# One stationary for the beta/decay projection, reordered opening transfers, chunk work by halves, and single row loads in the tail

## The chip, the cores and the metric

The kernel runs on one core of one Trainium2 chip. The metric is the device time of one execution in microseconds, the median of several runs. TensorE (PE) does matrix products into PSUM, VectorE (DVE), ScalarE (ACT) and GpSimd (POOL) do the elementwise work, SyncE (SP) issues transfers; ScalarE and GpSimd can issue transfers as well. Each engine works through its own queue in order, and a transfer that has to wait holds up all that stands behind it in the queue that issues it.

## What is computed

One layer of a hybrid decoder on 1024 prompt tokens and 8 x 4 sample tokens (1056 columns in all), model width 1024, 8 heads of 128. All is fp32. The parts that matter here:

```python
u = _rmsnorm(x, norm_w)
proj = jnp.einsum('btd,dn->btn', u, w_in)
a_b, a_c, a_h, a_z, qkv, b_z, b_beta, b_alpha, g_a, g_b = jnp.split(proj, _split_points(), axis=-1)
...
qkv_c, new_qkv_buf = _causal_conv(qkv, conv_qkv_buf, conv_b_w)      # width 4, per channel
qkv_c = jax.nn.silu(qkv_c).astype(jnp.float32)
...
beta = jax.nn.sigmoid(b_beta)
g = -jnp.exp(a_log) * jax.nn.softplus(b_alpha + dt_bias)
o, S_new = _gated_delta(q, k, v, beta, g, S0)                       # chunked; decays L, products k k^T and q k^T
...
m = jax.nn.sigmoid(g_a) * y_a + jax.nn.sigmoid(g_b) * y_b
return x + jnp.einsum('btd,de->bte', m, w_o), new_a_buf, new_qkv_buf, S_new
```

`b_beta` and `b_alpha` are 8 columns each, so the beta/decay projection has 16 columns where every other unit has 128.

## The kernel before

Every fp32 product is made of three products at reduced precision: each operand is split into a high part (`uh`, `wh`) and a low part (`ul`, `wl`), and `wh*uh + wl*uh + wh*ul` is accumulated (L286). A unit of the input projection is 128 weight columns: 8 row blocks x 3 products x 3 column blocks of 352 tokens, 72 matmuls. `fetch_plain` (L177) loads its weights on SP's queue, `prep` (L184) makes `wh` on ScalarE (L188) and `wl` on VectorE (L190). `take` (L212) prepares up to two units ahead and fetches up to four ahead, as the buffers allow (three raw weight tiles `wr`, four split tiles `hl`).

In the opening (L435 to L468) nine blocks of x rows are loaded on SP, squared on ScalarE, scaled with `nwb` (the norm weights on all partitions, loaded by a broadcast on ScalarE's queue, L437) on VectorE (L455), transposed on TensorE (L460) and split into `uh` and `ul`. Then come the beta/decay unit (BA) and the first key unit (k0), block by block in turn (L466), and the unpacking of BA (L471 to L567), which gives `beta`, the gates and their running sums. These go to DRAM (`gscr`, L546) and are read back per head by a broadcast, as `ee` and `qd` (L590, L594).

The head loop (L788) runs the convolution of k, q and v for each of eight heads: a projection, an evacuation by ScalarE (L404), edge columns by GpSimd (L411 to L414), and the taps on ScalarE and VectorE (L416, L418). `decay_matrices` (L596) turns `ee` into the decays: GpSimd (L599), VectorE (L600), ScalarE (L601). The work of a head on its chunks is the generator `chunk` (L715). `pump()` is called after each of the nine blocks of a head and takes one step of the chunk of the head before; `finish(fore)` runs what is left of it. `chunk` has ten steps: `qd` and two stores; the eight transposes of k with squares and scalings (L733, L734); the norms (`tk`, `al`, `bp`); the squares of q; and for each half the products (L756), the masks, the stores of `mm` into three scratch tensors (L768 to L774), the transposes of v and the store of `pk` (L784). The clearing stores of the scratch tensors (L801, 1 MB each) go out on SP two per head in heads 0 to 4.

Afterwards come the unit products of z, then pairs of units in a seven-product scheme (`project_pair`, L311), each pair 7 x 24 matmuls, with the inversion, the merge, the scan and the sample stage as `background` steps between the products. Ahead of the last gate pair (L1220) the background is run to its end, and five `y` rows are loaded at once on ScalarE's queue (L1226). The output projections follow.

The order in each queue is planned ahead by a scheduler that simulates the program's times, so instructions of neighbouring steps can change places. The plan is fixed when the program is built.

## Time and profile before

| | us |
|---|---|
| median of three runs | 1457.48 (1456.57 to 1462.76) |
| the profiled execution | 1458.91 |
| its span | 1457.2 |
| TensorE busy | 1393.4 (96%) |
| VectorE busy | 793.8 (54%) |
| ScalarE busy | 550.9 (38%) |
| GpSimd busy | 408.6 (28%) |

The span lies 1.7 us under the time of the execution. An engine's busy time counts its instructions, not its waits. The granted clock is the share of TensorE's full speed of 2.4 GHz: 1.00 is full speed, 0.50 is the lower level of 1.2 GHz. Matmuls overlap each other, so the duration of one is longer than its share of the time; how fast they follow is read from the time that a known number of them takes. "Queue" lines with a q behind the engine (SPq, ACTq) are the issue of a transfer, not the transfer.

### The profile page before, as it was taken

Reading aid. Unit: us, or ns where it says so; the run is one execution under the profiler, and the core shown is the slowest. Engines: PE = TensorE matmul, PEld = TensorE weight load, DVE = VectorE, ACT = ScalarE, POOL = GpSimd, SP = SyncE. Lnnn points to the kernel's source line nnn. Section 1 sums busy time; section 2 is a strip of 40 time slices with the busy share of each in tenths; the row PEclk is TensorE's granted clock in tenths of the full one; section 3 lists DMA queues with packets and bytes.
Section 4 is the critical chain, followed back from the end, with each engine's and each line's share of the span. In section 5 each row is a group of like instructions: output and inputs, shape, how many; then the busy total and the mean of one; then the engine's idle time right before and its main releaser. Section 6 shows DMA issues by size and latency. Waiting matters only on the chain.

```text
span 1457.2 us, 24544 instructions
## 1 busy us (share of the span) xinstructions
PE 1393.4 (96%) x9673; PEld 1339.5 (92%) x9673; DVE 793.8 (54%) x1456; ACT 550.9 (38%) x1184; POOL 408.6 (28%) x613
## 2 busy tenths in 40 slices
PE   4999898998999999899999999999999899999998
PEld 3899898998999999799999999999988899999785
DVE  6255543455438998455545566466676462355322
ACT  5165545555543443133334443442232440123111
POOL 2034323132211100475444565542253000001100
PEclk8999999999999999999999999999999999999999
DMA  6167755655546235944355776654446773333311
GB/s 202 29 141 205 188 164 171 195 135 145 135 136 152 87 106 128 227 91 120 81 144 156 212 201 196 183 161 124 116 134 196 256 247 100 103 118 109 142 44 47
DMA packets 229124, 212.33 MB, mean 146 GB/s; under 512 B 45801, under 2 KB 200314, under 8 KB 229010
## 3 DMA queue, kind: packets, MB, share of 16 engines
q1 hardware_dynamic: 204224, 139.91, 34.5%
q0 software_dynamic: 21712, 64.10, 15.0%
q10 hardware_dynamic: 3074, 6.77, 1.3%
q8 instruction: 76, 1.25, 0.3%
q14 instruction: 38, 0.31, 0.1%
HBM read 138.12 MB, written 72.56 MB: 145 GB/s over the span
## 4 chain that ended last, share of the span: by engine, by line
PE 68%; DMA 12%; DVE 11%; issue 3%; SPq 3%; POOL 1%; ACT 1%; DVEq 0%; POOLq 0%; ACTq 0%
PE pb L325 27%; PE pp L287 24%; PE pp L1319 6%; DMA ee<-gscr 6%; DMA wr<-in_w_in_dram 2%; DVE cv L418 2%; DMA sb<-in_state_delta_dram 1%; DVE wl L190 1%; DMA ya<-in_x_prompt_dram 1%; DVE xi L620 1%; PE pd L1021 1%; DVE pr L619 1%; PE po L1147 1%; PE pd L1145 1%; PE pd L756 1%
## 5 line engine op out<-in xcount | busy, mean ns | idle before, releaser
L325 PE MATMUL pb<-uh,w 128*128 128x264 f32 x1600 | 312.1, 292 | 12.1 <-ACT w L208 5.8
L325 PEld LDWEIGHTS pb<-uh,w 128*128 128x128 f32 x1600 | 253.5, 191 | 17.3 <-ACT w L208 7.2
L287 PE MATMUL pp<-uh,wl 128*128 128x352 f32 (+1 forms) x744 | 243.1, 327 | 14.0 <-DVE wl L190 14.0
L287 PE MATMUL pp<-uh,wh 128*128 128x352 f32 (+1 forms) x744 | 250.0, 336 | 3.3 <-ACT ext L406 3.3
L287 PE MATMUL pp<-ul,wh 128*128 128x352 f32 (+1 forms) x744 | 242.7, 326 | 0.0
L325 PE MATMUL pb<-ul,w 128*128 128x264 f32 x800 | 232.1, 290 | 0.0
L287 PEld LDWEIGHTS pp<-uh,wl 128*128 128x128 f32 (+1 forms) x744 | 139.9, 188 | 18.5 <-DVE wl L190 16.0
L325 PEld LDWEIGHTS pb<-ul,w 128*128 128x128 f32 x800 | 153.1, 191 | 1.7 <-issue 1.7
L287 PEld LDWEIGHTS pp<-uh,wh 128*128 128x128 f32 (+1 forms) x744 | 139.5, 188 | 7.3 <-ACT ext L406 3.7
L287 PEld LDWEIGHTS pp<-ul,wh 128*128 128x128 f32 (+1 forms) x744 | 139.8, 188 | 2.2
L208 ACT CAST w<-s 128x512 fp32r<-128x512 f32 x100 | 61.5, 620 | 139.1 <-PE pb L325 97.8
L418 DVE SCALAR_TENSOR_TENSOR cv<-ext,vecT,cv 128x1080 f32<-128x1080 f32 x72 | 99.7, 1388 | 9.7 <-ACT cv L416 8.3
L209 DVE TENSOR_TENSOR w<-s,w 128x512 fp32r<-128x512 f32 x100 | 72.2, 723 | 32.6 <-ACT w L208 32.2
L188 ACT CAST wh<-wr 128x1024 fp32r<-128x1024 f32 (+1 forms) x47 | 48.7, 1036 | 107.6 <-PE pp L287 105.2
L325 PE MATMUL pb<-t4h,w 128*128 128x264 f32 x400 | 78.8, 295 | 5.0 <-DVE p L858 5.0
L190 DVE TENSOR_TENSOR wl<-wr,wh 128x1024 fp32r<-128x1024 f32 (+1 forms) x47 | 59.8, 1272 | 37.3 <-ACT wh L188 36.2
L325 PE MATMUL pb<-t7h,w 128*128 128x264 f32 x400 | 77.6, 291 | 0.0
L325 PE MATMUL pb<-t6h,w 128*128 128x264 f32 x400 | 77.2, 289 | 0.0
L209 DVE TENSOR_TENSOR w<-wr,w 128x512 fp32r<-128x512 f32 x75 | 51.3, 686 | 45.2 <-ACT w L208 45.1
L325 PEld LDWEIGHTS pb<-t4h,w 128*128 128x128 f32 x400 | 64.2, 194 | 6.4 <-issue 6.4
L208 ACT CAST w<-wr 128x512 fp32r<-128x512 f32 x75 | 46.7, 623 | 52.5 <-PE pb L325 50.2
L331 ACT COPY p<-pb 128x528 f32<-128x528 f32 x50 | 30.0, 600 | 92.7 <-PE pb L325 92.7
(366 smaller groups left out, 3148.7 us busy)
## 6 DMA issues: line engine op xcount, KB each, us to landing
wr<-in_w_in_dram SPq DMA_DIRECT2D x80, 512.0 KB
scr<-pk SPq DMA_DIRECT2D x16, 768.0 KB
sb<-in_state_delta_dram POOLq DMA_DIRECT2D x16, 512.0 KB, 4.4
zscr<-zt SPq DMA_DIRECT2D x8, 528.0 KB
gbscr<-zt SPq DMA_DIRECT2D x8, 528.0 KB
yscr<-za SPq DMA_DIRECT2D x8, 528.0 KB
gascr<-zt SPq DMA_DIRECT2D x8, 528.0 KB
sg<-gascr POOLq DMA_DIRECT2D x8, 528.0 KB, 4.0
```

Of the source, the lines that this page charges most:

```text
L188: act.copy(wh, wr)
L190: dve.tensor_tensor(wl, wr, wh.bitcast(F32), op=ALU.subtract)
L208: act.copy(w2[:, 0], src)
L209: dve.tensor_tensor(w2[:, 1], src, w2[:, 0].bitcast(F32), op=ALU.subtract)
L287: pe.matmul(ps[:a.shape[2], :BLK], lhsT=a[:, k, :], rhs=m[k][:, sl], start=(k == 0 and i == 0), stop=(k == KC - 1 and i == 2))
L325: pe.matmul(ps[:, g, :QT], lhsT=a[:, k, :], rhs=m[:, k, sl], start=start and k == 0 and i == 0, stop=(k == 3 and i == 2), skip_group_check ...
L331: act.copy(t, ps)
L418: dve.scalar_tensor_tensor(cv, ext[:, j:j + LB], vecT[:, j * 24 + ci:j * 24 + ci + 1], cv, op0=ALU.mult, op1=ALU.add)
L619: dve.tensor_tensor(pv, xi[:, 0:j, 0:j], bc(dl[:, j, 0:j], 1, [P, j, j]), op=ALU.mult)
L620: dve.tensor_reduce(xi[:, 0:j, j], pv, axis=AX.X, op=ALU.add, negate=True)
L756: pe.matmul(pt[:, i * 256:(i + 1) * 256], lhsT=kq[:, 0, c * P:(c + 1) * P], rhs=kq[:, :, c * P:(c + 1) * P], start=True, stop=True)
L1319: pe.matmul(ps[:n, :], lhsT=a[k][:, sl], rhs=w[k][:, cs_], start=(k == 0 and i == 0), stop=(k == KC - 1 and i == 2))
```

## The change

Six things are changed. The weights of BA become one tile of 48 columns, with the high part in columns 0 to 15, zeros in 16 to 31 and the low part in 32 to 47; two products take the place of three, and the two results are added when BA is unpacked. The norm weights are loaded as one row and spread over the partitions by two products with `ones`. BA and k0 are taken without looking ahead; the next units are fetched behind the rows of x. `ee` and `qd` are loaded, and `mm` is stored, on GpSimd's queue (`aux`). `chunk` does all of one half before the other, in nine steps. The five `y` rows are loaded on GpSimd's queue, one per product of the last gate pair, by a new generator.

```diff
@@ -184,6 +184,12 @@
     def prep(u, j):
         if u[0] == "c":
             wr, n = rawc.pop(j) if j in rawc else fetch_plain(u)
+            if n == 16:
+                both = wp.tile([P, KC, 48], F32R, tag="hl", name="wb", bufs=4)
+                pool.memset(both[:, :, 16:32].bitcast(F32), 0.0)
+                act.copy(both[:, :, 0:16], wr)
+                dve.tensor_tensor(both[:, :, 32:48], wr, both[:, :, 0:16].bitcast(F32), op=ALU.subtract)
+                return both, None
             wh = wp.tile([P, KC, n], F32R, tag="hl", name="wh", bufs=4)
             act.copy(wh, wr)
             wl = wp.tile([P, KC, n], F32R, tag="hl", name="wl", bufs=4)
@@ -283,6 +289,11 @@
 
         def mm(ps, b, k):
             sl = slice(b * BLK, (b + 1) * BLK)
+            if wl is None:
+                for i, (n, m) in enumerate(((48, mh), (16, ml))):
+                    pe.matmul(ps[:n, :BLK], lhsT=wh[:, k, 0:n], rhs=m[k][:, sl], start=(k == 0 and i == 0),
+                              stop=(k == KC - 1 and i == 1), skip_group_check=True)
+                return
             for i, (a, m) in enumerate(((wh, mh), (wl, mh), (wh, ml))):
                 pe.matmul(ps[:a.shape[2], :BLK], lhsT=a[:, k, :], rhs=m[k][:, sl], start=(k == 0 and i == 0),
                           stop=(k == KC - 1 and i == 2))
@@ -394,7 +405,7 @@
     s_st, st = opened(name="st", bufs=1, side="right")
     s_y, pools["y"] = opened(name="xy", bufs=1, side="right")
 
-    def conv_begin(ci):
+    def conv_begin(ci, ahead=True):
         ext = qe.tile([P, EXB], F32, name="ext", bufs=2)
         sv = psel(ext, 3 + T, NT + 3, 3)
 
@@ -404,7 +415,7 @@
             act.copy(ext[:, 3 + lo:3 + lo + n], ps[:, :n])
             if b == NBLK - 1:
                 act.copy(sv[:, :, 3:7], ps[:, n:n + TS].rearrange("p (b t) -> p b t", t=NT))
-        mm, run = begin(w_in, C_Q + ci * P, uh, ul)
+        mm, run = begin(w_in, C_Q + ci * P, uh, ul, ahead)
         return ext, sv, run, evac
 
     def conv_end(ci, out, ext, sv):
@@ -433,14 +444,19 @@
         return xt
 
     xts = [load_x(0), load_x(1), load_x(2)]
+    nwr = st.tile([1, D], F32, tag="pq", name="nwr", bufs=2)
+    nc.scalar.dma_start(nwr, norm_w)
     nwb = ytile(7, (P, D))
-    nc.scalar.dma_start(nwb, norm_w[0].partition_broadcast(P))
-    _, run_ba = begin(w_in, C_BA, uh, ul)
-    ext_k0, sv_k0, run_k0, evac_k0 = conv_begin(8)
-    bar = st.tile([16, TT], F32, name="bar")
+    for i in range(2):
+        pt = dtile()
+        pe.matmul(pt, lhsT=ones[0:1, :], rhs=nwr[:, i * 512:(i + 1) * 512], start=True, stop=True)
+        dve.tensor_copy(nwb[:, i * 512:(i + 1) * 512], pt)
+    _, run_ba = begin(w_in, C_BA, uh, ul, False)
+    ext_k0, sv_k0, run_k0, evac_k0 = conv_begin(8, False)
+    bar = st.tile([48, TT], F32, name="bar")
 
     def evac_ba(b, ps):
-        act.copy(bar[:, b * BLK:(b + 1) * BLK], ps[:16, :BLK])
+        act.copy(bar[:, b * BLK:(b + 1) * BLK], ps[:48, :BLK])
 
     for tb in range(9):
         n = P if tb < 8 else TS
@@ -463,6 +479,9 @@
             pv = pt.rearrange("p (k t) -> p k t", t=P)[:, :, :n]
             act.copy(gh, pv)
             dve.tensor_tensor(gl_, pv, gh.bitcast(F32), op=ALU.subtract)
+    ready[pos[0]] = prep(units[pos[0]], pos[0])
+    for j in range(1, 3):
+        rawc[pos[0] + j] = fetch_plain(units[pos[0] + j])
     for b in range(NBLK):
         run_ba(b, evac_ba)
         run_k0(b, evac_k0)
@@ -473,9 +492,12 @@
     pt = dtile()
     for tb in range(9):
         n = P if tb < 8 else TS
-        pe.transpose(pt[:n, tb * 16:(tb + 1) * 16], bar[:, tb * P:tb * P + n], ident[:16, :16])
-    dve.tensor_copy(bat[:, 0:8, :], pt[:, 0:128].rearrange("p (t c) -> p t c", c=16))
-    dve.tensor_copy(bat[:TS, 8, :], pt[:TS, 128:144])
+        pe.transpose(pt[:n, tb * 48:(tb + 1) * 48], bar[:, tb * P:tb * P + n], ident[:48, :48])
+    bv_ = pt[:, 0:9 * 48].rearrange("p (t c) -> p t c", c=48)
+    dve.tensor_copy(bat[:, 0:8, :], bv_[:, 0:8, 32:48])
+    dve.tensor_copy(bat[:TS, 8, :], bv_[:TS, 8, 32:48])
+    dve.tensor_tensor(bat[:, 0:8, :], bv_[:, 0:8, 0:16], bat[:, 0:8, :], op=ALU.add)
+    dve.tensor_tensor(bat[:TS, 8, :], bv_[:TS, 8, 0:16], bat[:TS, 8, :], op=ALU.add)
 
 
     vraw = st.tile([P, P], F32, name="vraw")
@@ -587,11 +609,11 @@
 
     def load_ee(h):
         ee[h] = qp.tile([P, NCH, P], F32, name="ee", bufs=2)
-        nc.sync.dma_start(ee[h], gv[0, h].partition_broadcast(P))
+        aux.dma_start(ee[h], gv[0, h].partition_broadcast(P))
 
     def load_qd(h):
         qds[h] = qp.tile([P, NCH, P], F32, name="qd", bufs=2)
-        nc.sync.dma_start(qds[h], gv[1, h].partition_broadcast(P))
+        aux.dma_start(qds[h], gv[1, h].partition_broadcast(P))
 
     def decay_matrices(h):
 
@@ -717,13 +739,14 @@
         pool.tensor_tensor(qd, kq[:, 1, 0:T].rearrange("p (c f) -> p c f", f=P), qd, op=ALU.mult)
         nc.sync.dma_start(sview[h, 3], kq[:, 0, 0:T].rearrange("p (c f) -> p c f", f=P))
         nc.sync.dma_start(sview[h, 4], qd)
-        al = qp.tile([P, NCH], F32, name="al")
-        bp = qp.tile([P, NCH], F32, name="bp")
-        tk = qp.tile([P, NCH], F32, name="tk")
+        sq = qe.tile([P, LB], F32, tag="cv", name="sq", bufs=2)
+        act.activation(sq[:, 0:T], kq[:, 1, 0:T], AF.Square)
         jk = qp.tile([P, P], F32, name="jk", bufs=2)
-        pk = [qp.tile([P, 4, 3, P], F32, name="pk", bufs=2) for _ in range(2)]
-        yield
         for hf in range(2):
+            yield
+            cs_ = slice(hf * 4, (hf + 1) * 4)
+            al, bp, tk = (qp.tile([P, 4], F32, name=nm, bufs=2) for nm in ("al", "bp", "tk"))
+            pk = qp.tile([P, 4, 3, P], F32, name="pk", bufs=2)
             pt = dtile()
             for i in range(4):
                 c = hf * 4 + i
@@ -731,22 +754,18 @@
             for i in range(4):
                 c = hf * 4 + i
                 act.activation(jk, pt[:, i * P:(i + 1) * P], AF.Square, accum_out=ssqk[:, c, h:h + 1])
-                act.activation(pk[hf][:, i, 0, :], pt[:, i * P:(i + 1) * P], AF.Copy, scale=kd[:, c, h:h + 1])
-        yield
-        dve.tensor_scalar(tk, ssqk[:, :, h], EPS, None, op0=ALU.add)
-        pool.tensor_tensor(al, tk, mhalf, op=ALU.pow)
-        pool.tensor_tensor(al, al, beta[:, 0:8, h], op=ALU.mult)
-        dve.reciprocal(bp, tk)
-        dve.tensor_tensor(bp, bp, beta[:, 0:8, h], op=ALU.mult)
-        dve.scalar_tensor_tensor(ngam[:, :, h], bp, -1.0, egc[:, :, h], op0=ALU.mult, op1=ALU.mult)
-        sq = qe.tile([P, LB], F32, tag="cv", name="sq", bufs=2)
-        act.activation(sq[:, 0:T], kq[:, 1, 0:T], AF.Square)
-        yield
-        pt = dtile()
-        for c in range(NCH):
-            pe.matmul(pt[:, c:c + 1], lhsT=sq[:, c * P:(c + 1) * P], rhs=ones[:, 0:1], start=True, stop=True)
-        dve.tensor_scalar(qn[:, :, h], pt[:, 0:NCH], EPS, P * EPS, op0=ALU.add, op1=ALU.mult)
-        for hf in range(2):
+                act.activation(pk[:, i, 0, :], pt[:, i * P:(i + 1) * P], AF.Copy, scale=kd[:, c, h:h + 1])
+            if hf == 0:
+                pt = dtile()
+                for c in range(NCH):
+                    pe.matmul(pt[:, c:c + 1], lhsT=sq[:, c * P:(c + 1) * P], rhs=ones[:, 0:1], start=True, stop=True)
+                dve.tensor_scalar(qn[:, :, h], pt[:, 0:NCH], EPS, P * EPS, op0=ALU.add, op1=ALU.mult)
+            dve.tensor_scalar(tk, ssqk[:, cs_, h], EPS, None, op0=ALU.add)
+            pool.tensor_tensor(al, tk, mhalf[:, 0:4], op=ALU.pow)
+            pool.tensor_tensor(al, al, beta[:, cs_, h], op=ALU.mult)
+            dve.reciprocal(bp, tk)
+            dve.tensor_tensor(bp, bp, beta[:, cs_, h], op=ALU.mult)
+            dve.scalar_tensor_tensor(ngam[:, cs_, h], bp, -1.0, egc[:, cs_, h], op0=ALU.mult, op1=ALU.mult)
             mm = qp.tile([P, 4, P], F32, name="mm", bufs=2)
             for j in range(2):
                 yield
@@ -757,21 +776,20 @@
                               rhs=kq[:, :, c * P:(c + 1) * P], start=True, stop=True)
                 pv = pt.rearrange("p (i x f) -> p i x f", i=2, x=2)
                 c0 = hf * 4 + j * 2
-                dve.tensor_tensor(pk[hf][:, j * 2:j * 2 + 2, 2, :], pv[:, :, 1, :], ee[h][:, c0:c0 + 2, :], op=ALU.mult)
+                dve.tensor_tensor(pk[:, j * 2:j * 2 + 2, 2, :], pv[:, :, 1, :], ee[h][:, c0:c0 + 2, :], op=ALU.mult)
                 for i in range(2):
-                    dve.scalar_tensor_tensor(mm[:, j * 2 + i, :], pv[:, i, 0, :], bp[:, c0 + i:c0 + i + 1],
+                    dve.scalar_tensor_tensor(mm[:, j * 2 + i, :], pv[:, i, 0, :], bp[:, j * 2 + i:j * 2 + i + 1],
                                              ee[h][:, c0 + i, :], op0=ALU.mult, op1=ALU.mult)
-            pool.affine_select(out=pk[hf][:, :, 2, :], in_=pk[hf][:, :, 2, :], pattern=[[0, 4], [1, P]],
+            pool.affine_select(out=pk[:, :, 2, :], in_=pk[:, :, 2, :], pattern=[[0, 4], [1, P]],
                                compare_op=ALU.is_ge, fill=0.0, base=0, channel_multiplier=-1)
-            cs_ = slice(hf * 4, (hf + 1) * 4)
             g, hl = h // GH, h % GH
-            nc.sync.dma_start(mscr[g, cs_, hl].rearrange("c i j -> i c j"), mm)
+            aux.dma_start(mscr[g, cs_, hl].rearrange("c i j -> i c j"), mm)
             for b in range(2):
                 o = b * 64
-                nc.sync.dma_start(lmscr[g, cs_, hl * Q4:(hl + 1) * Q4, b, hl * Q4:(hl + 1) * Q4].rearrange("c i j -> i c j"),
+                aux.dma_start(lmscr[g, cs_, hl * Q4:(hl + 1) * Q4, b, hl * Q4:(hl + 1) * Q4].rearrange("c i j -> i c j"),
                                   mm[o + Q4:o + 64, :, o:o + Q4])
             o = (hl % 2) * 64
-            nc.sync.dma_start(m64scr[g, cs_, o:o + 64, hl // 2, o:o + 64].rearrange("c i j -> i c j"),
+            aux.dma_start(m64scr[g, cs_, o:o + 64, hl // 2, o:o + 64].rearrange("c i j -> i c j"),
                               mm[64:128, :, 0:64])
             yield
             pt = dtile()
@@ -780,8 +798,8 @@
                 pe.transpose(pt[:, i * P:(i + 1) * P], vt[:, c * P:(c + 1) * P], ident)
             for i in range(4):
                 c = hf * 4 + i
-                act.activation(pk[hf][:, i, 1, :], pt[:, i * P:(i + 1) * P], AF.Copy, scale=al[:, c:c + 1])
-            nc.sync.dma_start(scr[hf * 4:(hf + 1) * 4, :, h, 0:3, :].rearrange("c p x f -> p c x f"), pk[hf])
+                act.activation(pk[:, i, 1, :], pt[:, i * P:(i + 1) * P], AF.Copy, scale=al[:, i:i + 1])
+            nc.sync.dma_start(scr[hf * 4:(hf + 1) * 4, :, h, 0:3, :].rearrange("c p x f -> p c x f"), pk)
 
     load_ee(0)
     load_qd(0)
@@ -1208,6 +1226,11 @@
             yield from fn(pl)
             held.close()
 
+    def load_early(tiles):
+        for k, t in enumerate(tiles):
+            yield
+            aux.dma_start(t, yscr[k])
+
     background.append(chain())
     rate[0] = 2.5
     by_pair(C_BZ, 6, AF.Silu, put_z)
@@ -1222,9 +1245,10 @@
             finish(background)
             s_yo, yo = opened(name="yo", bufs=1, side="right")
             early = [yo.tile([P, TT], F32, name=f"y{k}") for k in range(5)]
-            for k in range(5):
-                nc.scalar.dma_start(early[k], yscr[k])
+            background.append(load_early(early))
+            rate[0] = 1.0
         by_pair(C_GA, h, AF.Sigmoid, lambda e, t: nc.sync.dma_start(gascr[e], t))
+    finish(background)
     s_a.close()
     s_u.close()
     s_h, ha = opened(name="ha", bufs=16)
```

## Rows read from the trace of the kernel before

**Rows 1.** TensorE's waits, whole span: line, releaser, us in total, times, longest.
```profile
PE pp L460 <- DVE ya L455: 14.4, 6, 9.6
PE pp L287 <- DVE wl L190: 14.0, 6, 4.4
...
PE pb L325 <- DVE p L858: 5.0, 1, 5.0
...
PE pp L287 <- ACT ext L406: 3.3, 1, 3.3
```

**Rows 2.** Three stretches: length, busy time of PE PEld DVE ACT POOL, clock, DMA, GB/s.
```profile
6.00:34.00 28.00, 15.44 (x73) 12.84 (x74) 22.89 (x36) 19.68 (x39) 6.14 (x10) 0.90 0.75 221
...
140.00:360.00 220.00, 203.18 (x1251) 198.65 (x1250) 102.05 (x143) 114.22 (x271) 58.77 (x99) 0.97 0.62 166
...
1100.00:1140.00 40.00, 34.63 (x246) 31.91 (x245) 24.30 (x57) 11.88 (x20) 9.11 (x9) 0.93 0.74 247
```

**Rows 3.** Chain of work that ended last: start, us, what; opening and head loop.
```profile
33.90 25.36 PE pp L287 x144
...
252.41 6.08 PE pp L287 x23
...
263.64 3.83 PE pp L287 x24
```

**Rows 4.** All engines' waits between 184 and 206 us.
```profile
POOL ee L599 <- DMA ee<-gscr: 17.1, 1, 17.1
...
ACT pk L734 <- DMA scr<-pk: 7.2, 1, 7.2
DVE ee L600 <- POOL ee L599: 6.2, 1, 6.2
```

**Rows 5.** Timeline around 204 us: start, us, instruction, idle time before it and releaser.
```profile
203.83 1.23 DVE L600 SCALAR_TENSOR_TENSOR ee<-ee 128x1024 f32<-128x1024 f32 x1 [6.22 <-POOL ee L599]
...
204.97 1.22 DVE L190 TENSOR_TENSOR wl<-wr,wh 128x1024 fp32r<-128x1024 f32 x1
...
206.25 0.43 PE L287 MATMUL pp<-uh,wl 128*128 128x352 f32 x1 [1.41 <-DVE wl L190]
```

**Rows 6.** Timeline of SP's queue ahead of the same stall.
```profile
184.23 0.61 SPq L801 DMA_DIRECT2D llscr<-zer  x1
184.96 0.59 SPq L784 DMA_DIRECT2D scr<-pk  x1
185.59 3.47 SPq L590 DMA_DIRECT2D ee<-gscr  x1
```

**Rows 7.** What the DMA engines moved from 177 to 202 us, in 40 slices.
```profile
GB/s 401 398 392 360 338 252 71 0 13 88 92 88 88 93 83 59 89 167 269 372 399 419 415 402 388 403 380 288 36 85 61 75 74 107 127 105 133 89 142 202
```

**Rows 8.** GpSimd's DMA issues, ns min/median/max: L965 with its landing, then L682.
```profile
L965 POOL DMA_DIRECT2D sb<-in_state_delta_dram x16: 882/887/948, 987.2 to 1116.5; - x16
...
DMA to landing us min/median/max: 4.2/4.4/8.8
...
L682 POOL DMA_DIRECT2D tscr<-xx x32: 687/693/796, 598.1 to 649.8; - x32
```

**Rows 9.** Waits of SP's queue between 60 and 440 us, one of them.
```profile
SPq L594 <- DMA scr<-qd: 22.5, 6, 4.5
```

**Rows 10.** First use of `nwb`; a PSUM copy; a 512-column fp32 product (two instructions).
```profile
8.22 1.28 DVE L455 SCALAR_TENSOR_TENSOR ya<-ya,rs,ya 128x1024 f32<-128x1024 f32 x1 [0.67 <-POOL rs L454]
...
84.32 0.69 DVE L563 COPY gsb<-pd 128x512 f32<-128x512 f32 x1
...
L990 PE MATMUL pd<-dg,ones x2: 592/592/592, 998.7 to 999.1; 128*128 128x512 f32 x2
```

**Rows 11.** Last gate pair: chain of work (first line), then the timeline.
```profile
1126.84 6.66 DMA wr<-in_w_in_dram
...
1126.50 0.89 POOL L1098 DMA_DIRECT2D out_dram<-sb  x1 [1.78 <-DVE sb L1096]
...
1128.66 1.00 ACTq L1226 DMA_DIRECT2D y<-yscr  x2
```

## What was predicted

> **What bounds the kernel now.** I read the share of busy time on the page first: TensorE is busy 96% of the span, so a change gains only by taking away TensorE work or by closing the stretches in which it waits or runs at the low clock. So the next view is what TensorE waits for [rows 1], then the stretches in which that happens [rows 2], and for each stretch who makes it wait.
>
> Three stretches matter here. In the **opening** (6 to 34 us) TensorE transposes the normalised rows and waits for VectorE [rows 1]; VectorE is busy 22.89 of 28.00 us [rows 2], so it nearly bounds that stage itself, with 5.1 us of slack. In the **head loop** (140 to 360 us) TensorE is busy 203.18 of 220 us [rows 2], and the 16.8 us missing are the waits for `wl` and for `ext` [rows 1]. After some of these waits the clock is low too: 23 matmuls take 6.08 us where 24 otherwise take 3.83 [rows 3]. The granted clock over that stretch is 0.97 [rows 2], which is worth up to 0.03 x 220 = 6.6 us more. I count the stretch as 16.8 + about 6 = 23 us lost. In the **tail of the gate projections** (1100 to 1140 us) 5.4 us are idle and the clock is 0.93 [rows 2], 7 us or so in all, nearly all of it at one wait of 5.0 us [rows 1].
>
> Why the head loop stalls is read backwards. TensorE waits 1.41 us for `wl`; VectorE made `wl` (L190) directly behind the `ee` step (L600), which it could start only at 203.83 [rows 5]. L600 waited 6.2 us for GpSimd's L599, which waited 17.1 us for the load of `ee` [rows 4]. The weights had long been there; `wl` merely stood behind L600 in VectorE's queue. The load was issued at 185.59 right behind a 1 MB clearing store and a 768 KB `pk` store on the same queue [rows 6]. The rate of the DMAs in that stretch shows it [rows 7]: 40 slices of 0.625 us, about 400 GB/s while the stores go through (to about 195 us), then about 100 GB/s for the last 7 us, which is the 512 KB of `ee` alone (0.1 MB/us x 7 us is 0.7 MB). So of 16.2 us some 9.5 are queueing and 7 the transfer. In the same period ScalarE waits 7.2 us for a `pk` store to land before it may write the next `pk` [rows 4].
>
> **The change part by part.**
>
> *Beta/decay projection.* 72 matmuls (3 blocks x 8 x 3) become 48, since one 48-column stationary does the high and the low part at once. A matmul here streams the same 352 columns whatever the width of the stationary, and the BA and k0 matmuls together take 25.36 us for 144 [rows 3], 0.176 each with the slow start in it. 24 fewer are worth 24 x 0.16 = 3.8 us at the full clock and 4.2 us at that mean. TensorE goes from block to block there without a gap, so all of it is on the path. I take 3.8. What is added (a memset on GpSimd, two adds in the unpacking of `bat`, wider transposes) runs beside the k0 and Q0 products.
>
> *Opening transfers.* Three 512 KB weight loads move behind the x rows, and the 512 KB broadcast of the norm weights becomes a 4 KB load, two products with `ones` and two copies. Fewer bytes stand ahead of x, but x is not the main limit: at most VectorE's 5.1 us of slack can be won. Against it: two 512-column fp32 products, two passes each, of about 0.4 us start to start at the high clock, hence twice that at the low clock, and two copies of 0.69 [rows 10]. At the low clock that is 4 x 0.8 + 0.7 = 4 us behind the 4 KB load, while the first use of `nwb` is at 8.22 now [rows 10]; so it could be up to 1 us late. Bounds -1 (a loss) to 5; I take 2, nearer to the lower end, because VectorE's own work stays as it is.
>
> *Loads of `ee` and `qd`, stores of `mm` to GpSimd's queue.* Per head that adds ten DMA instructions there: two like the 512 KB state loads at 0.89 us, eight at about 0.7 [rows 8], 7.4 us in 44. GpSimd is busy 58.77 of 220 us [rows 2]; five heads add 37, which makes 44%. The instruction time is covered. The state loads, same size and row length, land in 4.2 to 8.8 us, median 4.4 [rows 8]; `ee` took about 7 once it moved [rows 7]. So I put it at 7 to 9 us from issue instead of 16.2, 7 to 9 us sooner. The waits to be covered are at most 4.4 us each [rows 1]. So L600 comes early enough and `wl` with it. What GpSimd now has to wait for: `qd`'s load needs the store of the old `qd` to have landed, for which SP waited 22.5 us in 6 heads [rows 9]. Behind it on GpSimd stand the edge copies of the convolution (L411, L412), behind those ScalarE's L416 and VectorE's L418. 4 us there is inside the slack: a projection takes 3 x 3.83 = 11.5 us and the cast and `wl` need 2.3, so about 9 us are free.
>
> The Trainium skill speaks against this part (DMA: Bandwidth & Descriptors, section Issuing engines are not separate DMA queues): DMAs of all issuing engines run on the same 16 DMA engines, and another issuer saves only the issue time. By that rule `ee` would land no sooner and this term would be near 0; it is the first rival below. The trace here bears it out only where the engines are full: one state load took 8.8 us against a median of 4.4 [rows 8].
>
> *Chunk products half by half.* No operation of size is added: the small ones on `tk`, `bp`, `al` are done twice at half width (about 1 us more on VectorE and GpSimd per head, beside TensorE's 41). Each half's `pk` is now written six steps after the store that frees it rather than two or three, so the 7.2 us for `scr<-pk` [rows 4] go, and the VectorE wait behind them. The chunk needs one step fewer, so the last half no longer falls into the burst at the end of the head. TensorE does not wait for these, so I cost this at nothing and credit it with nothing on its own: it makes it likelier that the 23 us go.
>
> Head loop together: of 23 us I leave 4 for the `ext` wait (3.3 [rows 1]) and what is next late, and take 19; bounds 0 and 23.
>
> *Rows one to a product.* In the tail the weight load for the second half of the last pair was issued at 1126.84 and took 6.66 us; the `sb` store had been issued at 1126.50, and at 1128.66 the first two of five 528 KB `y` loads on ScalarE's queue came in [rows 11]. In the change they come one per product on GpSimd's queue, the first two products later. Without 1 MB of them at about 370 GB/s (2.6 MB between 1126.5 and 1133.5) the weights could land 2 to 3 us sooner. That leaves 2 to 3 us of the 5.0 wait, since the `sb` store stays, and so does the load for the next projection behind it. I take 3 with the clock; bounds 0 and 7. The last `y` is asked for about 18 us into a pair of some 20 and lands before its cast, which comes 10 us later.
>
> Sum: 3.8 + 2 + 19 + 3 = 27.8. The profiled execution took 1458.9 us (span 1457.2), 1.4 above the median of 1457.5, so 1431.1 against it and 1429.7 against the median. I write 1430.
>
> **The rivals.**
> *A, the queue is not what holds `ee`.* If the transfers share the engines so that `ee` still ends with the burst, or VectorE is held by something else, the 19 go and the rest stays: 1457.5 - 8.8 = 1449, with a part of them 1443 to 1453. For it: the engines move 400 GB/s in that burst [rows 7]. Against it: the burst ends 7 us before `ee` lands, and the state loads take 4.4 [rows 8].
>
> *B, GpSimd's queue becomes the blocker; slower.* `qd`'s load waits for the store of the old `qd`, and all of GpSimd behind it. It decides from about 9 us of waiting per head. If the store lands after a burst like that of rows 7 (9.5 + 4.5 = 14 us), each of seven heads loses 5 us and 2 for the clock, 49 instead of 23: 1457.5 + 26 - 8.8 = 1475. Against it: the wait is under 4.5 each time now [rows 9], and the burst gets smaller. The Trainium skill has a second reason (SBUF - State Buffer, section SBUF: two separate sides): descriptors written by GpSimd can be held up by VectorE. No sign of it here: the issue times stay within 882 to 948 ns [rows 8] beside a VectorE that is busy half the time.
>
> *C, more goes than I count*: the whole 23, 5 of the opening and 7 of the tail, 1457.5 - 38.8 = 1419. The order in each queue is planned anew for the whole program, so stalls after 440 us, which the change does not touch, can move by a few us either way in all cases.
>
> **How the numbers follow.** Forecast 0.66 (1422 to 1441, when 14 to 23 of the head loop go), A 0.20, B 0.06, C 0.08. The range 1419 to 1450 leaves out B and a part of A, about 0.15. 0.5% is about what can be told from no change here, 7.3 us: faster is below 1450.2. That is the forecast, C and half of A or more, 0.66 + 0.08 + 0.12 = 0.86; same 0.08; slower 0.06.
>
> **What the profile after would show.** The waits of TensorE for `wl` in the head loop nearly gone and the granted clock there at 1.00; GpSimd's wait for `ee` (17.1) under 8 us a head; ScalarE's wait for `scr<-pk` gone; 48 matmuls in the beta/decay projection and the end of the k0 projection some 6 us earlier; the wait at the last pair below 3. The prediction is wrong if GpSimd's waits for `scr<-qd` grow past 9 us, or if `ee` still takes 14 us or more from its issue.

## The result, and the profile after

The changed kernel takes 1438.02 us (median of 3 runs, 1435.91 to 1439.44) against 1457.48 us: a ratio of 0.986, interval 0.983 to 0.988. Its profiled execution has a span of 1436.3 us, 20.9 less than before. The forecast was 1430. The time lies inside the range and inside the forecast's own band of 1422 to 1441, 8 us above the forecast. The ratios further down are to other runs of the kernel before, with medians of 1458.45 to 1459.97 us. So a total that misses a band by 1 to 3 us says little, and the readings go by stages and waits.

TensorE's waits over the whole span (the view of [rows 1]: line, releaser, us in total, times, longest):

```profile
PE pb L336 <- ACT w L214: 9.3, 2, 5.6
PE pp L476 <- DVE ya L471: 9.2, 4, 5.0
...
PE pb L336 <- DVE za L965: 5.2, 1, 5.2
...
PE pb L336 <- DVE p L876: 1.8, 1, 1.8
...
PE pd L761 <- ACT sq L743: 0.4, 1, 0.4
```

The 14.0 us for `wl` and the 3.3 us for `ext` are gone, and all that is left of waits between 60 and 440 us is the last line. Of the 9.3 us in the first line 5.6 are a wait late in the pairs that before had 5.5 us (L325 then); the other 3.7 are new: the first of the unit pairs (L336, formerly L325) waits for its weights.

The stretches of [rows 2], and 440 to 480 us beside them (length, busy time of PE PEld DVE ACT POOL, clock, DMA, GB/s):

```profile
6.00:34.00 28.00, 15.19 (x76) 12.84 (x76) 24.05 (x39) 20.03 (x38) 6.93 (x10) 0.81 0.73 205
...
140.00:360.00 220.00, 220.00 (x1400) 217.21 (x1399) 118.01 (x181) 124.13 (x291) 109.97 (x171) 1.00 0.65 171
...
440.00:480.00 40.00, 35.48 (x249) 34.97 (x248) 39.50 (x107) 17.49 (x32) 4.07 (x4) 0.91 0.20 68
...
1100.00:1140.00 40.00, 38.23 (x315) 38.04 (x314) 18.84 (x38) 16.02 (x27) 6.41 (x10) 1.00 0.76 257
```

In the head loop TensorE is busy without a gap at a granted clock of 1.00 (before 203.18 of 220 us at 0.97). Between 440 and 480 us it now loses 4.5 us and the clock falls to 0.91, with VectorE busy 39.50 of 40 us.

The opening of the chain of work that ended last (start, us, what), to be read beside the first line of [rows 3]:

```profile
33.34 4.36 PE pp L294 x16
37.70 3.84 PE pp L298 x24
41.54 2.56 PE pp L294 x16
```

A block of the beta/decay projection is now 16 products in 2.56 us. All the stages, from the starts of the main products in the trace (us; opening: to the first main product; head loop: first Q product to the first `z` product; there are 25 pairs):

| kernel | opening | BA and k0 | head loop | z | pair 1 | pairs 2 to 19 | pairs 20 to 25 | output | span |
|---|---|---|---|---|---|---|---|---|---|
| before | 33.8 | 26.8 | 341.1 | 76.5 | 20.9 | 494.1 | 169.5 | 294.5 | 1457.2 |
| after | 33.3 | 22.5 | 318.0 | 76.6 | 28.0 | 497.3 | 167.6 | 293.0 | 1436.3 |
| q_only | 34.1 | 25.9 | 322.9 | 76.5 | 21.7 | 497.5 | 171.9 | 294.2 | 1444.7 |
| ch_only | 34.2 | 26.5 | 320.3 | 76.7 | 22.8 | 498.3 | 173.2 | 294.2 | 1446.3 |
| ee_back | 33.4 | 23.1 | 321.0 | 76.6 | 27.4 | 496.2 | 164.9 | 294.1 | 1436.7 |
| mm_back | 33.3 | 22.0 | 328.7 | 76.6 | 24.1 | 494.6 | 163.7 | 293.9 | 1436.9 |
| open_act | 35.0 | 22.4 | 318.1 | 76.6 | 27.8 | 498.3 | 167.7 | 293.9 | 1439.9 |
| open_old | 33.7 | 22.9 | 318.7 | 76.6 | 27.8 | 500.2 | 165.7 | 293.0 | 1438.7 |
| open_late | 33.1 | 22.9 | 317.9 | 76.6 | 28.2 | 495.2 | 166.4 | 294.1 | 1434.6 |
| y_once | 33.5 | 23.3 | 319.5 | 76.6 | 27.6 | 497.3 | 171.6 | 294.2 | 1443.6 |
| tok_pool | 33.4 | 23.1 | 319.5 | 76.6 | 33.5 | 495.5 | 163.8 | 293.5 | 1439.0 |
| chain_late | 33.9 | 22.2 | 317.9 | 76.6 | 27.8 | 481.3 | 171.6 | 304.6 | 1435.9 |
| late2 | 33.1 | 22.8 | 318.7 | 76.6 | 27.8 | 480.8 | 172.2 | 305.1 | 1437.1 |
| inv_dep | 33.4 | 22.2 | 319.1 | 76.6 | 26.6 | 506.3 | 176.7 | 293.5 | 1454.4 |

From before to after: opening -0.6, beta/decay -4.4, head loop -23.1, `z` +0.1, first pair +7.1, pairs 2 to 19 +3.2, pairs 20 to 25 -1.8, output -1.6; together -21. Each row is one execution. The kernels that differ from after only in the opening (open_act, open_old, open_late) show how far a stage moves when nothing in it was edited: pairs 2 to 19 lie between 495 and 500 us (497 in after), so 3 us in that column are not read as an effect. In the same way BA and k0 take 22.0 to 23.3 us in the eleven kernels with 48 products, and pairs 20 to 25 take 163.7 to 167.7 us in the seven kernels whose chain and `y` loads are those of the changed kernel (inv_dep, chain_late and late2 move the chain).

### The profile page after: what moved, and what is told of

It reads as the page before. It is cut to its first block, busy times and chain, and to the rows that moved or that the text cites. A ratio compares the mean times of both kernels' runs of the same rounds, so it can differ in the third digit from the quotient of the medians.

```text
span 1436.3 us, 24538 instructions
## 1 busy us (share of the span) xinstructions
PE 1391.0 (97%) x9653; PEld 1339.6 (93%) x9653; DVE 796.5 (55%) x1492; ACT 553.7 (39%) x1186; POOL 483.5 (34%) x715
## 4 chain that ended last, share of the span: by engine, by line
PE 83%; DVE 6%; DMA 6%; issue 1%; SPq 1%; ACT 1%; POOL 1%; DVEq 0%; POOLq 0%; ACTq 0%
PE pp L298 36%; PE pb L336 27%; PE pp L1343 7%; DMA wr<-in_w_in_dram 2%; PE pd L775 2%; DMA sb<-in_state_delta_dram 2%; PE pd L1039 1%; PE pd L761 1%; DVE w L215 1%; PE po L1165 1%; PE pd L1163 1%; PE pd L1156 1%; PE po L1145 1%; PE pd L1143 1%; DVE xi L642 1%
## 5 line engine op out<-in xcount | busy, mean ns | idle before, releaser
L336 PE MATMUL pb<-uh,w 128*128 128x264 f32 x1600 | 315.3, 294 | 17.0 <-ACT w L214 9.3
L336 PEld LDWEIGHTS pb<-uh,w 128*128 128x128 f32 x1600 | 256.9, 194 | 21.3 <-ACT w L214 9.7
L298 PE MATMUL pp<-uh,wh 128*128 128x352 f32 x720 | 240.6, 334 | 0.0
L336 PE MATMUL pb<-ul,w 128*128 128x264 f32 x800 | 233.9, 292 | 0.0
L298 PE MATMUL pp<-ul,wh 128*128 128x352 f32 x720 | 232.1, 322 | 0.0
L298 PE MATMUL pp<-uh,wl 128*128 128x352 f32 x720 | 231.4, 321 | 0.0
L336 PEld LDWEIGHTS pb<-ul,w 128*128 128x128 f32 x800 | 155.3, 194 | 1.2 <-issue 1.2
L298 PEld LDWEIGHTS pp<-uh,wl 128*128 128x128 f32 x720 | 135.6, 188 | 1.6 <-issue 0.8
L298 PEld LDWEIGHTS pp<-uh,wh 128*128 128x128 f32 x720 | 135.2, 188 | 1.2
L298 PEld LDWEIGHTS pp<-ul,wh 128*128 128x128 f32 x720 | 135.3, 188 | 0.0
L196 DVE TENSOR_TENSOR wl<-wr,wh 128x1024 fp32r<-128x1024 f32 x46 | 59.8, 1301 | 64.5 <-ACT wh L194 46.9
L194 ACT CAST wh<-wr 128x1024 fp32r<-128x1024 f32 x46 | 48.5, 1055 | 114.8 <-PE pp L298 110.1
L336 PE MATMUL pb<-t4h,w 128*128 128x264 f32 x400 | 79.5, 296 | 1.8 <-DVE p L876 1.8
L336 PE MATMUL pb<-t7h,w 128*128 128x264 f32 x400 | 76.8, 289 | 0.0
L336 PE MATMUL pb<-t6h,w 128*128 128x264 f32 x400 | 76.5, 288 | 0.0
L336 PEld LDWEIGHTS pb<-t4h,w 128*128 128x128 f32 x400 | 63.8, 193 | 3.9 <-issue 3.6
```

The lines of the kernel that those rows point to most:

```text
L194: act.copy(wh, wr)
L196: dve.tensor_tensor(wl, wr, wh.bitcast(F32), op=ALU.subtract)
L298: pe.matmul(ps[:a.shape[2], :BLK], lhsT=a[:, k, :], rhs=m[k][:, sl], start=(k == 0 and i == 0), stop=(k == KC - 1 and i == 2))
L336: pe.matmul(ps[:, g, :QT], lhsT=a[:, k, :], rhs=m[:, k, sl], start=start and k == 0 and i == 0, stop=(k == 3 and i == 2), skip_group_check ...
```

## The experiments

**Which part freed the head loop.** Four kernels take the two parts of the head loop apart.

q_only, the kernel before with the queues alone changed:

```diff
-        nc.sync.dma_start(ee[h], gv[0, h].partition_broadcast(P))
+        aux.dma_start(ee[h], gv[0, h].partition_broadcast(P))
...
-            nc.sync.dma_start(mscr[g, cs_, hl].rearrange("c i j -> i c j"), mm)
+            aux.dma_start(mscr[g, cs_, hl].rearrange("c i j -> i c j"), mm)
```

> The kernel before with one part of the change: the loads of ee and qd and the stores of mm go to GpSimd's queue; chunk products, opening, beta/decay projection and tail as before. Theory Q (the stall came from ee queued behind SP's stores): TensorE's waits for wl between 60 and 440 us fall from 14.0 to under 4 us, ee lands 12 to 14 us after its issue instead of 16, and of the 23 us of the head loop some 16 to 19 go, less up to 8 given back at the first pair: 1440 to 1447. Rival H (the order of the chunk's steps is what freed VectorE's queue, the queue change alone is not enough): wl waits stay at 10 us or more, 1452 to 1458. Rival B (GpSimd's queue turns into the blocker without the new chunk order): SP's old waits for scr<-qd show up on GpSimd at 4 us or more a head, 1458 or above.

1445.46 us, ratio 0.992 (0.989 to 0.995). Waits of 60 to 440 us (same columns as above, chosen lines):

```profile
ACT pk L734 <- DMA scr<-pk: 35.4, 5, 11.3
POOL qd L594 <- DMA scr<-qd: 25.9, 5, 8.0
...
PE pp L287 <- DVE wl L190: 4.0, 2, 3.6
```

The head loop shrinks by 18.2 us and 4.0 us of waiting for `wl` stay, just at the edge of theory Q, which held in its other sizes. Part of rival B is here too: GpSimd now waits for `scr<-qd`, 8.0 us at the longest (SP waited 4.5 at the longest [rows 9]), close to the 9 us from which it would have cost time.

ch_only, the kernel before with the chunk products half by half and nothing else:

```diff
-        pk = [qp.tile([P, 4, 3, P], F32, name="pk", bufs=2) for _ in range(2)]
-        yield
         for hf in range(2):
+            yield
...
+            pk = qp.tile([P, 4, 3, P], F32, name="pk", bufs=2)
```

> The kernel before with one part of the change: chunk products half by half; ee, qd and mm stay on SP's queue. Theory Q: ee still lands 15 to 17 us after its issue, wl waits of 9 to 14 us in the head loop remain, 1450 to 1458. Rival H: wl waits under 4 us, 1438 to 1445. In both ScalarE's wait for scr<-pk (7.2 in one head) should go.

1447.97 us, ratio 0.994 (0.992 to 0.996). TensorE's waits of 60 to 440 us:

```profile
PE pp L287 <- ACT ext L406: 1.3, 1, 1.3
PE pp L287 <- DVE wl L190: 0.4, 1, 0.4
```

The head loop shrinks by 20.8 us with `ee` still on SP's queue. Rival H held for the waits, against theory Q; the total is worse than H's 1438 to 1445 by 3 us. ScalarE's wait for `scr<-pk`, 42.0 us in five heads before, has no line left. And `ee` lands sooner without having changed its queue: in heads 2 to 7 GpSimd can begin on it 9.4 to 12.0 us after its issue, against 15.4 to 16.9 us in heads 1 to 6 before. SP's queue shows why in the head of [rows 6]: the `pk` store and the clearing store, which before were issued 0.6 and 1.4 us ahead of `ee`, now go out 11 us ahead of it:

```profile
166.27 0.38 SPq L780 DMA_DIRECT2D scr<-pk  x1
166.70 0.55 SPq L797 DMA_DIRECT2D llscr<-zer  x1
...
177.51 1.46 SPq L590 DMA_DIRECT2D ee<-gscr  x1
```

ee_back, the changed kernel with only `ee` and `qd` back on SP's queue (`aux.dma_start` to `nc.sync.dma_start` in the two loads):

> The changed kernel with only the loads of ee and qd back on SP's queue (the mm stores stay on GpSimd's). Theory Q: ee lands 15 us or more after its issue and the waits for wl come back, 8 us of them or more: 1446 to 1456. Rival H: no waits for wl above 2 us, within 3 us of the changed kernel (1435 to 1441).

1442.48 us, ratio 0.990 (0.987 to 0.993); 1.5 us above rival H's band and under theory Q's. The head loop is 321.0 and no wait for `wl` comes back, which is H. SP's queue and GpSimd's row of one head:

```profile
166.88 0.36 SPq L612 DMA_DIRECT2D ee<-gscr  x1
167.75 0.36 SPq L741 DMA_DIRECT2D scr<-qd  x1
177.31 0.36 SPq L616 DMA_DIRECT2D qd<-gscr  x1
```

```profile
175.02 2.76 POOL L621 TENSOR_TENSOR ee<-ee,gc 128x1024 f32<-128x1024 f32 x1 [5.04 <-DMA ee<-gscr]
```

Issue 166.88, landed by 175.02: 8.1 us (8.0 to 9.5 in heads 2 to 7). In the changed kernel the same load on GpSimd's queue takes 12.5:

```profile
174.12 0.92 POOL L612 DMA_DIRECT2D ee<-gscr  x1
175.02 0.90 POOL L616 DMA_DIRECT2D qd<-gscr  x1
...
186.66 1.92 POOL L621 TENSOR_TENSOR ee<-ee,gc 128x1024 f32<-128x1024 f32 x1 [6.56 <-DMA ee<-gscr]
```

Two things run beside it there that come later in ee_back: the 512 KB of `qd`, 0.9 us behind `ee` (10 us in ee_back), and a `pk` store and a clearing store that SP issues at 171.62 and 172.31 (in ee_back the `pk` store is issued at 178.54, behind the load). Which of them lengthens the load is not separated. So once the stores are spread out, `ee` lands sooner in the kernel that has it on SP's queue; that the queue itself is the reason is not shown.

mm_back, the changed kernel with only the four `mm` stores back on SP's queue:

> The changed kernel with only the four stores of mm back on SP's queue (ee and qd stay on GpSimd's). Theory Q: the head loop stays free of waits (under 2 us in 60 to 440 us), and where VectorE waits 4.1 us for dl<-mscr near 425 us the wait changes with the place of the mscr stores; total within 4 us of the changed kernel (1434 to 1442). Rival S (it was the mm stores that held SP's ring up for pk and the state loads): waits of TensorE of 5 us or more come back in the head loop, 1443 or more.

1440.80 us, ratio 0.989 (0.986 to 0.992), inside theory Q's total, but not with a free head loop:

```profile
PE pd L798 <- ACT vt L431: 7.4, 5, 2.4
PE pd L761 <- ACT sq L743: 0.3, 1, 0.3
```

TensorE waits 7.4 us for `vt`, and the loop takes 328.7 us. Rival S's wait did come (by another tile than it named), and the rest of the span made up for it. ch_only, which also has its `mm` stores on SP's queue, doesn't wait like this, so these stores alone are not the cause. VectorE's wait for `dl<-mscr` fell to 1.3 us at most, and the first pair takes 24.1 us instead of 28.0.

**The first pair.** tok_pool puts the sums of the high and low parts on GpSimd:

```diff
-            dve.tensor_tensor(t, ug[g][0][:, k, lo:lo + HT].bitcast(F32), ...
+            pool.tensor_tensor(t, ug[g][0][:, k, lo:lo + HT].bitcast(F32), ...
```

> The changed kernel with the 16 additions of the token sums (high and low part, 128x528, 0.62 us start to start on VectorE, 9.9 us in all) on GpSimd, where one should take about 1.0 us (its 128x1024 subtraction takes 1.92). Theory V (VectorE, busy without a gap from 430 to 482 us, bounds the first pair, which takes 28.0 us instead of 20.9): the first pair shortens to 20 to 24 us and the time falls by 4 to 7 us (1431 to 1434). Rival P (weights or ScalarE bound it; or GpSimd's additions become the late step): first pair still 26 us or more, within 2 us of the changed kernel or slower.

1440.72 us, ratio 0.988 (0.986 to 0.990). The first pair grew to 33.5 us. An addition takes 1.55 us on GpSimd, not the 1.0 that was assumed:

```profile
L374 POOL TENSOR_TENSOR r<-uh,ul x16: 1293/1548/2766, 420.8 to 455.9; 128x528 f32<-128x528 f32 x16
```

The token sums end at 465.0 us, 12 us past TensorE's arrival. That shows that a later end of the token sums lengthens the pair (rival P's last clause); whether VectorE's load is to blame in the changed kernel it leaves open.

chain_late starts the chain with the inversion one pair later:

```diff
-    background.append(chain())
-    rate[0] = 2.5
     by_pair(C_BZ, 6, AF.Silu, put_z)
+    background.append(chain())
+    rate[0] = 2.5
```

> The changed kernel with one edit: the background chain that begins with the inversion (16 us of small VectorE steps beside the first pair) starts one pair later. Theory V (VectorE without a gap from 430 to 482 us sets the end of the first pair near 478 to 481 us, whenever TensorE arrives there): the first pair takes 21 to 23 us instead of 28.0. If nothing later is near its limit the time falls by 4 to 7 us (1431 to 1434). Rival G (given back later): the first pair shortens as much, but pairs 3 to 19 grow by as much, time within 2 us of the changed kernel. Rival P (weights or ScalarE bound the first pair): it still takes 26 us or more.

1439.34 us, ratio 0.986 (0.984 to 0.989). The first pair takes 27.8 us, but the edit did not reach it. The first step of the inversion on VectorE:

```profile
429.86 0.16 DVE L641 TENSOR_TENSOR pr<-xi,dl 128x1 f32<-128x1 f32 x1 [3.97 <-DMA dl<-mscr]
```

In the changed kernel it starts at 429.70: the order on the engines is planned anew from dependencies and costs, and the planner put the inversion where it had been. What did move is later: pairs 2 to 19 are 16 us shorter, and at the end of the pairs TensorE waits for the gates' products instead, so the output stage is 11.6 us longer:

```profile
PE pp L298 <- ACT yh L1261: 6.7, 1, 6.7
PE pp L298 <- ACT zt L874: 4.5, 1, 4.5
```

inv_dep forces the order with a dependency:

```diff
+        pool.tensor_copy(xi[0:1, 0, 0:1], tok[5][1][0:1, 3, 0:1].bitcast(F32))
         pool.memset(xi, 0.0)
```

> The changed kernel with one edit: the inversion's start tile is first written from the last token sum, so that none of its steps can be placed ahead of the token sums on VectorE (the earlier edit, which moved it only in program order, left it at the same 429.9 us). Theory V (VectorE bounds the first pair: its token sums are 31.2 us of work, and in their midst it waits 4.1 us for dl and does 2.7 us of inversion): the token sums end some 6 us earlier, the first pair takes 21 to 24 us instead of 28.0, and the time falls by 4 to 7 us (1431 to 1434). Rival G (given back later, the inversion and what hangs on it now being late): the first pair shortens as much, pairs 2 to 19 grow by as much. Rival P (weights or ScalarE bound the first pair): it still takes 26 us or more.

1445.16 us, ratio 0.991 (0.989 to 0.993); the profiled execution took 1456.2, 11 us more, so its late stages are not read to the microsecond. The inversion begins at 456.6 us, the wait for `dl` is gone, and yet the first pair takes 26.6 us: theory V's 21 to 24 falls, and rival P's figure holds. VectorE, at the end of the token sums:

```profile
453.67 0.68 DVE L204 TENSOR_TENSOR s<-wr 128x512 f32<-128x512 f32 x1
455.59 0.71 DVE L380 TENSOR_TENSOR t4l<-r,t4h 128x528 fp32r<-128x528 f32 x1 [1.24 <-ACT t4h L379]
456.57 0.37 DVE L642 TENSOR_TENSOR pr<-xi,dl 128x1 f32<-128x1 f32 x2 [0.28 <-POOL xi L636]
```

The sums end 5.0 us after TensorE's arrival instead of 7.5: of the 6.8 us taken out of VectorE's queue (4.1 of waiting, 2.7 of inversion) 2.5 reach the end, for the sums now wait for ScalarE's casts in turn (1.2 us here). So theory V's first step failed: the sums didn't end 6 us earlier. The later pairs are longer (+9 and +9 us), but in an execution 11 us over the median, so rival G is not shown by it.

**The opening.** open_old takes the opening transfers back to those of before (broadcast of the norm weights, three weight loads first):

> The changed kernel with the opening transfers as before (512 KB broadcast of the norm weights, three weight loads ahead of the fourth row block), and the rest of the change kept. If the opening transfers are worth only the 0.55 us seen between the starts of the projections (33.83 and 33.27), projections start at 33.5 to 34.2 and the time is within 1.5 us of the changed kernel. If the reordering is worth the 2 us of the prediction, it is 1.5 to 4 us slower.

1439.86 us, ratio 0.987 (0.985 to 0.989): projections start at 33.7 instead of 33.3. The reordering is worth about half a microsecond: the four kernels with the old opening start at 33.7 to 34.2, the seven with the new one unedited at 33.3 to 33.9. open_act puts the two copies of the norm weights on ScalarE (`dve.tensor_copy(nwb...)` to `act.copy(nwb...)`):

> The changed kernel with one edit: the two copies of the norm weights from PSUM to nwb are on ScalarE instead of VectorE. Theory C (the second copy stands in VectorE's queue behind the mean square of the second row block, so the first scaling step starts at 9.72 instead of some 7 us, and VectorE bounds the opening): the first scaling step starts at 7.0 to 8.0, projections start at 31 to 32 instead of 33.27, 1.5 to 2.5 us less in all. Rival W (ScalarE's queue, held by the casts of the fetched weights near 11 and 16 us, bounds it): first scaling step earlier, but projections start within 0.7 us of 33.27.

1441.84 us, ratio 0.989 (0.987 to 0.991). Projections start at 35.0, later than either theory allowed. But ScalarE's second copy came only at 9.60 us and the first scaling at 10.26 instead of 9.72, so the earlier scaling that both theories start from never came, and neither is tested. ScalarE then waited longer for the weights than in the changed kernel (3.58 us against 1.19):

```profile
15.61 1.04 ACT L194 CAST wh<-wr 128x1024 fp32r<-128x1024 f32 x1 [3.58 <-DMA wr<-in_w_in_dram]
```

open_late casts the first two weights only ahead of the seventh row block:

> The changed kernel with one edit in the opening: the beta/decay and first key weights are fetched as early, but cast to their two parts only ahead of the seventh row block, not ahead of the first. Theory W (ScalarE, in whose queue the casts stand and which waits for these weights near 11 and 15.9 us, holds row blocks 4 to 9 up): TensorE's longest wait of 5.0 us in the opening shortens by 2 us or more, projections start at 31.5 to 32.5 instead of 33.27. Rival V2 (VectorE, idle for 1.5 us only between 9.7 and 34 us, bounds the opening): projections start within 0.7 us of 33.27.

1440.99 us, ratio 0.987 (0.985 to 0.990), projections at 33.1: rival V2. TensorE's longest wait there fell by 1.0 us (5.0 to 4.0; it is 4.9 in late2, which has the same edit) and the end stayed. late2 has open_late's and chain_late's edits together:

> Both of the two edits in one kernel. By theories V and W together 1429 to 1433; by rival G or P with V2 1436 to 1441. The two touch stretches 400 us apart, so the start of the projections should be that of the one and the first pair's length that of the other, within 1 us.

1439.04 us, ratio 0.986 (0.983 to 0.989): by rival P with V2, and each stage is as long as in the kernel that has its edit alone, within 1 us.

**The last pair.** y_once issues the five `y` loads on ScalarE's queue as before:

> The changed kernel with the five loads of y issued at once on ScalarE's queue, as before. If they were what delayed the second half of the last pair's weights, the wait there of 1.8 us becomes 4 to 5.5 us and the time grows by 3 to 5 us (1441 to 1443). If other traffic delayed it, the wait stays under 3 us and the time within 1.5 us.

1445.22 us, ratio 0.991 (0.989 to 0.993). Pairs 20 to 25 are 4.0 us longer than after. The wait of TensorE at the last pair, and the weight load that it hangs on, from the chain of work:

```profile
PE pb L336 <- DVE p L876: 4.4, 1, 4.4
```

```profile
1111.67 9.23 DMA wr<-in_w_in_dram
```

In the changed kernel the wait is 1.8 us and the load takes 5.18:

```profile
1111.14 5.18 DMA wr<-in_w_in_dram
```

The first theory held for the wait; the time is 2 us above its band. No kernel of this study is faster than the changed one by more than the intervals.

## Why the prediction was right or wrong

*Beta/decay projection.* Forecast 3.8, measured 4.4. 24 products at 0.16 (2.56 us for 16) are the 3.8. The rest lies in the slow start, which takes 4.36 us for the first 16 products and changes from kernel to kernel: the stage is 25.9 to 26.8 us in the three kernels with 72 products and 22.0 to 23.3 in the eleven with 48, 3.7 apart in the mean. So the forecast was right, and the 0.6 above it is spread.

*Opening.* Forecast 2, measured 0.6 (0.4 by open_old). The term was mis-sized. The products for `nwb` were as slow as written (3.75 us), but on VectorE the second copy stands behind the second mean square, and the third, for which VectorE waits 0.96 us, stands ahead of the first scaling. That starts at 9.72 us, 1.5 later than [rows 10]; the bound had 1 us:

```profile
5.83 0.68 DVE L453 COPY ya<-pd 128x512 f32<-128x512 f32 x1
7.89 0.15 DVE L468 TENSOR_SCALAR ms<-ss 128x1 f32<-128x1 f32 x1 [1.38 <-ACT ya L466]
7.96 0.68 DVE L453 COPY ya<-pd 128x512 f32<-128x512 f32 x1
9.60 0.15 DVE L468 TENSOR_SCALAR ms<-ss 128x1 f32<-128x1 f32 x1 [0.96 <-ACT ya L466]
9.72 2.48 DVE L471 SCALAR_TENSOR_TENSOR ya<-ya,rs,ya 128x1024 f32<-128x1024 f32 x2
```

From there to the first projection (33.3) VectorE is idle for 1.5 us only, so rows that land sooner gain next to nothing. The 5.1 us of slack that the prediction counted were not all slack: some 2 of them lay ahead of the first scaling at 8.22, and from there VectorE was busy 22.64 of 25.70 us before the change too.

*Head loop.* Forecast 19, measured 23.1, all of it. The stall was read rightly: `wl` behind the `ee` step, `ee` behind the burst of stores. Three statements about the cure were not. First, moving the loads to GpSimd's queue does not make `ee` land in 7 to 9 us; it takes 12.5 to 14 in heads 2 to 7, with `qd` right behind it and stores on SP's queue beside it; the state loads were the wrong row to size it by, and the last 7 us of [rows 7] were not `ee` alone (SP issued a weight load at 189.28, behind it). That was enough, because the stall needed only some 4 us. In the head of [rows 5], VectorE now idles even longer for `ee`, and it costs nothing:

```profile
188.62 1.22 DVE L622 SCALAR_TENSOR_TENSOR ee<-ee 128x1024 f32<-128x1024 f32 x1 [9.03 <-POOL ee L621]
...
190.61 1.22 DVE L196 TENSOR_TENSOR wl<-wr,wh 128x1024 fp32r<-128x1024 f32 x1
```

The projection that needs this `wl` starts at 194.0, 2.2 us after it is done. Second, the chunk products were costed "at nothing" and credited "with nothing on its own"; alone they take 20.8 us off the loop, by spreading the stores, and ee_back shows that with them the queue of `ee` hardly matters (3 us of the loop). Third, the wait for `scr<-qd` was said to stay under 4.5 us; with the queue change alone it reached 8.0, and it is the chunk order that keeps it harmless:

```profile
POOL ee L621 <- DMA ee<-gscr: 53.4, 7, 8.5
...
POOL qd L616 <- DMA scr<-qd: 1.4, 1, 1.4
```

So each part by itself cures most of the stall and the gains do not add: 18.2 and 20.8 alone, 23.1 together. The Trainium skill's rule on issuing engines (DMA: Bandwidth & Descriptors, section Issuing engines are not separate DMA queues) would have left `ee` where it was. q_only speaks against that in effect (12.1 to 13.5 us from issue to use in heads 2 to 6, 15.4 to 16.9 before), ee_back for it: with the burst gone, `ee` lands no sooner from another issuer.

The signs that the prediction named came: no wait for `wl`, the granted clock at 1.00, GpSimd's wait for `ee` at 7.6 us a head (8.5 at the longest), ScalarE's for `scr<-pk` gone, 48 products in the beta/decay projection and the end of the k0 projection 5 us earlier (54.3 against 59.3). One of its signs of being wrong came as well: `ee` took 15.5 and 26.1 us from issue to use in heads 0 and 1, whose loads are issued at 76.2 and 78.9 us. TensorE didn't wait for that, so a late `ee` was a poorer sign than the prediction took it for.

*Tail.* Forecast 3, measured 4.0 by y_once; the wait is 1.8 us, and 4.4 to 5.4 in the four kernels with the old `y` loads (before, q_only, ch_only, y_once). The reason held (the load of the weights takes 5.18 us, 9.23 with the `y` loads on ScalarE's queue), though the loads do not come one to a product: the planner issues the five between 1111.09 and 1115.54 us. From before to after the stage as a whole gained only 1.8, but that is one execution of each: it takes 169.5 to 173.2 us in the four kernels with the old loads and 163.7 to 167.7 in the seven with the new ones, so the gain is clear and its size is not.

*What was missing.* With the measured sizes the terms give 4.4 + 0.6 + 23.1 + 4.0 = 32.1, and the span fell by 20.9. Of the 11 us between, 7.1 were lost at the first pair, 3.2 in pairs 2 to 19, and 2.2 in pairs 20 to 25 (4.0 by y_once, 1.8 by the stage); 1.6 came back in the output stage. The step that failed is the clause that the change does not touch the stalls after 440 us. It does, at the first pair. First token sum and first product of the pair (line, count, ns, first and last start), before and after:

```profile
L363 DVE TENSOR_TENSOR r<-uh,ul x16: 687/694/714, 441.0 to 473.2; 128x528 f32<-128x528 f32 x16
...
L325 PE MATMUL pb<-uh,w x1600: 278/284/687, 478.3 to 1158.7; 128*128 128x264 f32 x178
```

```profile
L374 DVE TENSOR_TENSOR r<-uh,ul x16: 695/702/714, 418.3 to 452.3; 128x528 f32<-128x528 f32 x16
...
L336 PE MATMUL pb<-uh,w x1600: 278/284/687, 450.4 to 1139.3; 128*128 128x264 f32 x178
```

From the first sum to TensorE's arrival VectorE had 37.2 us before and has 32.1 now, for sums that take it 31.2 us by themselves. The profiled kernels fall into two groups: 37 us with the old chunk order (before, q_only), 32 us with the new one (the other twelve), whatever the queues. So the chunk order, costed at nothing, takes 5 us of VectorE's time here; that the reason is its last half, whose transposes, products and stores now follow on one another at the end of the loop, is argued, not shown. In the midst of the sums VectorE also waits 4.1 us for `dl`, which the inversion reads back from the scratch tensor of `mm`:

```profile
424.91 0.71 DVE L380 TENSOR_TENSOR t7l<-t,t7h 128x528 fp32r<-128x528 f32 x1
429.70 0.16 DVE L641 TENSOR_TENSOR pr<-xi,dl 128x1 f32<-128x1 f32 x1 [4.08 <-DMA dl<-mscr]
429.78 0.70 DVE L394 TENSOR_TENSOR r<-r,r 128x528 f32<-128x528 f32 x1
```

The sums end at 457.9, 7.5 us after TensorE arrives (2.5 before), and the weights of the pair stand behind them. TensorE stops twice, and the granted clock falls to 0.84 and 0.82 in the ten-microsecond stretches from 450 and 460 us:

```profile
457.18 0.59 PE L336 MATMUL pb<-uh,w 128*128 128x264 f32 x1 [3.69 <-ACT w L214]
458.59 0.59 PE L336 MATMUL pb<-uh,w 128*128 128x264 f32 x1 [0.83 <-DVE w L215]
```

That is 4.5 us of waiting and some 3 of clock. The shorter time for the sums is not the whole cause, though: ch_only has the same 32 us and its pair is only 1.9 us longer than before. The first pair in eight kernels (us; VectorE's longest wait for `dl` among the sums, the end of the sums after TensorE's arrival, TensorE's waits within the pair, and its granted clock there, from the traces):

| kernel | first pair | wait for `dl` | sums end after arrival | TensorE waits | granted clock |
|---|---|---|---|---|---|
| before | 20.9 | 0.3 | 2.5 | 0.2 | 1.00 |
| q_only | 21.7 | 0.9 | 3.5 | 0.9 | 1.00 |
| ch_only | 22.8 | 1.6 | 4.4 | 1.8 | 1.00 |
| mm_back | 24.1 | 1.3 | 4.0 | 1.5 | 0.93 |
| inv_dep | 26.6 | 0 | 5.0 | 3.4 | 0.87 |
| ee_back | 27.4 | 3.9 | 7.4 | 4.8 | 0.94 |
| after | 28.0 | 4.1 | 7.5 | 4.5 | 0.88 |
| tok_pool | 33.5 | 0 | 12.3 | 9.6 | 0.80 |

The later the sums end, the longer the pair, apart from mm_back, whose clock falls where that of ch_only doesn't. The queues alone cost 0.8 us (q_only). The new chunk order with the `mm` stores on SP's queue costs 1.9 to 3.2 us (ch_only, mm_back); with these stores on GpSimd's queue it costs 6.5 to 7.1, whichever queue `ee` is on (ee_back, after). So the loss needs both parts, and some 4 us of it go with the queue of the `mm` stores, after which VectorE waits 4 us for `dl` instead of 1.3 to 1.6; why `dl` lands later then is not shown. Taking the wait away by moving the inversion brings only 1.3 us back (inv_dep), because the sums then wait for ScalarE's casts; how the rest divides between VectorE's sums and these casts stays open. Of the +3.2 us in pairs 2 to 19 no cause is shown; the kernels that were not edited there spread by as much.

*The total.* The mechanism of the head loop held and its stall went whole. That 1438 lies in the band of 1422 to 1441 is luck in part: with 14 to 23 us from the head loop and 8.8 from the rest, the prediction's own sum gives 1426 to 1435. The named terms gained 4 us more than was forecast, and 11 us went where the prediction had nothing.

## What to carry to other kernels

A stall can have several cures, each nearly enough by itself, and their gains then do not add: look for what bunches the transfers before moving one of them to another queue. And when a stage in front gets shorter, work out for the next stage how long its slow engine has between its earliest start and TensorE's arrival, and what it waits for in that time. Here 5 us less of it cost 1.9 alone (ch_only), and 7.1 together with a move of stores to another queue, after which that engine waits 4 us for a load; the terms themselves had gained 32. Where a planner sets the order, an edit of program order may not move anything, so read the engine's own order before drawing a conclusion.

## What the runs showed of the hardware

A 512 KB broadcast load (`ee`) took 8.0 to 9.5 us from its issue to its use on SP's queue with the stores spread out (ee_back, heads 2 to 7), 12.5 to 14 us on GpSimd's queue with the load of `qd` close behind it (after, heads 2 to 7), and 15.4 to 16.9 us on SP's queue behind a burst of stores (before, heads 1 to 6; 1.8 MB of them in the head of [rows 6]), while the 512 KB state loads take 4.4 [rows 8]: size alone doesn't give the time of a load. An addition of two 128x528 tiles took 1.55 us on GpSimd in the median (1.29 to 2.77, tok_pool) and 0.62 start to start on VectorE, though GpSimd does a 128x1024 subtraction in 1.92 (after; up to 2.92 in ee_back): its time can't be scaled from one row to another shape.
